# One VectorE instruction per modulation block, a later gate-bias scaling, and a fixed reuse order for two single buffers

## The chip, the cores and the metric

The kernel runs on one NeuronCore of a Trainium2 chip. The metric is the time of one execution in microseconds of device time. The median of three runs of the kernel before is 3478.86 us (3476.70 to 3480.21).

TensorE (PE in the profile) does matrix products and transposes, VectorE (DVE) and ScalarE (ACT) elementwise work, GpSimd (POOL) a little elementwise work, and SyncE (SP) issues nearly all transfers between HBM and the on-chip memory. Each engine runs its own instructions in the order in which they were written.

## The reference

Two networks follow each other on one sequence of 512 tokens with 1024 features. The first has two layers of: a hybrid mixer (branches A and B are attention, branch C is spatial gating), cross attention to a memory, and a convolutional feed-forward. The second has two layers with a mixer and an MLP each; both are wrapped in a modulation computed from a vector `c`. What the change touches:

```python
def window_attention(...):            # branch A; B is the dense form without the band
    p = jax.nn.softmax(jnp.concatenate([s, sink_l], axis=-1), axis=-1)[..., :-1]
    o = jnp.einsum('bnkgqs,bnskd->bnqkgd', p, vw)

def hybrid_mixer(...):
    gates = jax.nn.sigmoid(gate + b_gate)              # b_gate is the gate bias
    merged = (jnp.einsum('bsnc,ncd->bsnd', branches, w_branch) * gates).sum(axis=2)

def sandwich(x, c_act, sublayer, g_pre, g_post, w_mod, b_mod):
    shift, scale, gate = jnp.split(c_act @ w_mod + b_mod, 3, axis=-1)
    h = rms_norm_2(x, g_pre) * (1 + scale) + shift
    return x + gate * rms_norm_2(sublayer(h), g_post)
```

`c_act @ w_mod` is a row vector of 1024 numbers times a matrix of 1024 x 3072, four times (two layers, two sublayers each). `diff_attention`, in the first mixer of the second network, subtracts one softmax from another for each of eight heads.

## The kernel before

**Precision.** Almost every product is done in three passes: weights and activations are each split into a high part (`whi`, `fTh`, a reduced format) and the rest (`wlo`, `fTl`), and three matmuls of 128 x 512 add up hi x hi, hi x lo and lo x hi (`mm3`). A weight block of 128 x 1024 numbers arrives by DMA in `raw` (three buffers); ScalarE copies it to `whi`, VectorE subtracts to get `wlo` (`split_block`; six buffers of each).

**Order.** The kernel is traced through a recording layer (`Line`, L133 to L279) that keeps an estimate of when each engine is free and each tile ready. `defer` puts a piece of work on a heap with the estimated time at which its inputs are ready, and `poll`, called after every triple of matmuls, runs what is due. So the instruction order of every engine follows from the estimated costs in `cost` (L262): a VectorE `scalar_tensor_tensor` is booked at 0.13 us + n/960, a GpSimd elementwise operation at 0.07 us + n/460. `pump` splits weight blocks ahead of their use as long as VectorE is not booked too far ahead. All instructions pass through one helper line, so the profile puts them all on L186.

**The modulation** (`mod_load`, `mod_step`, `mod_go`, L1274 to L1330) is worked off inside the two feed-forwards (`conv_ffn`), 48 blocks in each: every up-projection of the feed-forward triggers one or two steps. A step takes one block of 128 x 1024 numbers of the matrix (`mraw`, three buffers, loaded two steps ahead). For the first of eight blocks ScalarE writes `macc = mraw * c`. For the other seven ScalarE scales `mraw` in place by a number per partition and GpSimd adds it to `macc`. After the eighth, `sums` has TensorE add up the 128 partitions with a matrix of ones (`macc,ones`), twelve times in all.

**The gate bias.** `hybrid` loads `bg` (128 x 24) and halves it on VectorE at once. Its first use is the `Tanh` in `branch`, after branch C and the projections of branch A.

**Attention of branches A and B, and the sliding window later** (`launch`, `probs_out`). Sixteen units run in pairs; each pair turns its probabilities (`sc`) by TensorE transposes into `pt0` and `pt1`, one buffer each, and then multiplies them by the values (`pv`). Nothing in the plan orders the turning of one pair after the `pv` of the pair before. In the same way `diff` has one buffer `qkl` for the low part of a head's keys, which the score products of the head read.

Of the kernel before, what the change touches and what calls it, by code (L numbers as in the profile page):

```python
# [14 lines left out]
AF = mybir.ActivationFunctionType  # L15
# [288 lines left out]
class KB:  # L304
# [460 lines left out]
    def probs_out(self, pool, u):  # L765


        nc, sh = self.nc, u.shared
        if not sh:
            sh["pt"] = [self.tile(pool, (P, u.wide // P, 2, P), f"pt{e}") for e in range(2)]  # L770
            sh["ev"] = Event(2, lambda: self.defer(0, pv, *sh["pt"]))
        for e in range(2):
            pp = self.ps((P, 4, P))
            self.transpose4(pp, [u.sc[e][:, b * P:b * P + P] for b in range(u.nkb)])
            pt = sh["pt"][e][:, :u.nkb, u.pr, :]
            if e == 0:
                nc.scalar.activation(pt, pp[:, :u.nkb, :], AF.Copy)
            else:
                nc.vector.tensor_copy(pt, pp[:, :u.nkb, :])
        u.read.set()  # L780

        def pv():
            po = self.ps((P, 2 * P))
            vc = slice(64 * u.kv, 64 * u.kv + 64)
            for b in range(u.nkb):
                for e in range(2):
                    nc.tensor.matmul(po[64 * e:64 * e + 64, :], lhsT=u.v[:, u.b0 + b, vc],
                                     rhs=sh["pt"][e][:, b, :, :].rearrange("p r q -> p (r q)"),
                                     start=b == 0, stop=b == u.nkb - 1)
            self.poll()  # L790
            sl, k = slice(u.i * P, u.i * P + P), 2 * u.kv
            self.split(u.br.h[:, k:k + 2, sl], u.br.l[:, k:k + 2, sl], po.rearrange("p (r q) -> p r q", r=2))

        sh["ev"].set()

# [55 lines left out]
    def launch(self, pool, unit, step, br, **kw):  # L851


        units, depth = [], kw["bufs"] // 2

        def start(n):
            if n >= depth and not units[n - depth].read.done:
                units[n - depth].read.after(lambda: self.defer(0, lambda: start(n)))
                return
            unit(pool, units[n])  # L860

        for n in range(16):
            kv, i, pr = n // 8, n // 2 % 4, n % 2
            u = Unit(kv=kv, i=i, pr=pr, shared={} if pr == 0 else units[-1].shared, br=br, read=Event(),
                     **{k: v for k, v in kw.items() if k != "band"})
            u.b0, u.nkb, u.add = kw["band"](i)
            units.append(u)
            self.defer(n * step, lambda n=n: start(n), kw["kh"], kw["kl"])


    def hybrid(self, l, xT):
        nc, A = self.nc, self.A
        with self.pool("hp") as hp:
            W = Weights(self, "w_in", l)
            WB = Weights(self, "w_branch", l)
            bg = self.load(hp, A["b_gate"][l], (P, 24), "bg")
            nc.vector.tensor_scalar_mul(bg, bg, 0.5)
            mg = self.tile(hp, (P, KD, S), "mg")

            def branch(n, br, first, done=None):  # L880
                wb = None
                for m in range(KD):
                    c = n * 8 + m
                    ps = self.dense(W.next(), 0, xT, KD)
                    gt = self.tile(hp, (P, S), "gt", 2)
                    nc.scalar.activation(gt, ps, AF.Tanh, bias=bg[:, c:c + 1], scale=0.5)
                    if m % 2 == 0:
                        wb = WB.next()
                    ps = self.dense(wb, (m % 2) * P, br, 4, keep=m % 2 == 0)
                    if first:  # L890
                        nc.vector.scalar_tensor_tensor(mg[:, m, :], gt, 1.0, ps, op0=ALU.add, op1=ALU.mult)
                    else:
                        nc.vector.scalar_tensor_tensor(gt, gt, 1.0, ps, op0=ALU.add, op1=ALU.mult)
                        nc.vector.tensor_tensor(mg[:, m, :], mg[:, m, :], gt, op=ALU.add)
                    if done:
                        done(m)

            def new_br():
                return FT(*self.pair(hp, (P, 4, S), "br", 2))

            brc = new_br()
            with self.pool("cp") as cp:
                self.branch_c(cp, l, xT, W, brc)
                self.flush()
            bra = new_br()
            with self.pool("ap") as ap, ExitStack() as es:
                self.branch_ab(es, ap, l, xT, W, bra, "a")
                branch(2, brc, True)
                self.flush()
            brb = new_br()  # L910
            with self.pool("ap") as ap, ExitStack() as es:
                self.branch_ab(es, ap, l, xT, W, brb, "b")
                branch(0, bra, False)
                self.flush()
            with self.pool("mt") as mt:
                hi, lo = self.pair(mt, (P, KD, S), "mT")
                mT = FT(hi, lo, (), [Event() for _ in range(KD)])

                def merged(m):
                    def go():  # L920
                        self.split(hi[:, m, :], lo[:, m, :], mg[:, m, :], scale=0.5)
                        mT.ev_k[m].set()
                    self.defer(0, go, mg[:, m, :])

                branch(1, brb, False, merged)
                self.flush_to_k(mT)
                self.open_boundary(self.open_right(), A["ln1_g"], A["ln1_b"], l)
                WM = Weights(self, "w_mix_out", l)
                fT, after = self.ln_start()
                self.tok(WM, mT, KD, 512, lambda t, ps: self.residual(t, 0, ps), by_k=True)  # L930
                self.tok(WM, mT, KD, 512, lambda t, ps: (self.residual(t, 1, ps), after(t)))
        return fT
# [356 lines left out]
    def mod_go(self):  # L1289
        nc, i = self.nc, self.mod_todo[0]  # L1290
        if not self.planning and nc.ready(self.mod_raw[i]) > self.now():
            self.defer(0, self.mod_go, self.mod_raw[i])
            return
        self.mod_todo.pop(0)
        s, kind, k = self.mod_steps[i]
        self.mod_load(i + 2)
        raw = self.mod_raw.pop(i)
        ck = self.cact[:, k:k + 1]
        if k == 0:
            self.mod_acc = self.tile(self.mod_pool, (P, D), "macc", 2)  # L1300
            nc.scalar.activation(self.mod_acc, raw, AF.Copy, scale=ck)
        else:
            nc.scalar.activation(raw, raw, AF.Copy, scale=ck)
            nc.gpsimd.tensor_tensor(self.mod_acc, self.mod_acc, raw, op=ALU.add)
        if k == KD - 1:
            acc, row = self.mod_acc, self.mod_sums[kind][s]

            def sums():
                ps = self.ps()
                for j in range(4):  # L1310
                    self.mm(ps[32 * j:32 * j + 32, 0:256], self.ones[:, 0:32], acc[:, 256 * j:256 * j + 256], 256)
                r = self.tile(self.mod_pool, (P, 256), "msum", 2)
                nc.scalar.activation(r, ps[:, 0:256], AF.Copy)
                nc.sync.dma_start(row.rearrange("(j c) -> j c", j=4), r[0:128:32, :])
                if c_last:
                    self.mod_finish(self.mod_pool)
                self.mod_left.set()

            c_last = i == len(self.mod_steps) - 1
            self.defer(0, sums, acc)  # L1320
# [415 lines left out]
    def diff(self, dp, hT, W, v, yT):  # L1736
        nc, A = self.nc, self.A
        sub = self.load(dp, A["e_diff_norm"], (P, 1), "sub")
        nc.vector.tensor_scalar_mul(sub, sub, 1.0 - LAM_INIT)

        def head(h):
            T = self.tile(dp, (P, 512), "T", 2)
            self.toeplitz(T, h, 0, 512)
            qk = []
            shared = {}

            def unit(i):
# [3 lines left out]
                for m in range(2):  # L1751
# [3 lines left out]
                    nc.vector.tensor_tensor_reduce(s, ps[:, :Wd], T[:, 384 - i * P:512], 1.0, NEG,  # L1755
                                                   ALU.add, ALU.max, mx[:, m:m + 1])
                    s2.append(s)
                nc.vector.tensor_scalar_mul(nm_, mx, -1.0)
                for m in range(2):
                    nc.scalar.activation(s2[m], s2[m], AF.Exp, bias=nm_[:, m:m + 1], accum_out=sums[:, m:m + 1])  # L1760
# [49 lines left out]
            def ev(i, ps):  # L1810
                t = self.tile(dp, (P, 2, S), f"qk{i}", 2, F32R)
                qk.append(t)
                if i == 0:
                    self.stack_q([t[:, e, :] for e in range(2)], ps, HD ** -0.5)
                else:
                    qk.append(self.tile(dp, (P, 2, S), "qkl", 1, F32R))
                    self.stack_k(t, qk[2], ps)
                    for n in range(NT):
                        self.defer(2.0 * n, lambda n=n: unit(n), *qk)
# [294 lines left out]
```

## Time and profile before

| quantity | before |
|---|---|
| median of three runs | 3478.86 us |
| the profiled execution, its own time | 3478.01 us |
| its span, first to last instruction | 3476.2 us |
| PE busy | 3366.9 us (97%) |
| DVE busy | 2078.5 us (60%) |
| ACT busy | 1433.7 us (41%) |
| POOL busy | 347.3 us (10%) |
| granted TensorE clock, mean | 0.987 of full |

The span is 1.8 us shorter than the execution's own time, and that execution lies within 0.03% of the median. "Busy" counts time in which at least one instruction of the engine is in flight. A row of the waits says which engine stood idle, for which tile it was released, and by whose work. "PEclk" is the share of TensorE's full clock that was granted in a stretch: 1.00 is 2.4 GHz, 0.50 is 1.2 GHz.

### The profile page before, as it was taken

To read this page: it belongs to the slowest core of one execution; us is meant where nothing else is said; L and a number is where in the kernel's file an instruction comes from. 1 tells how busy PE (TensorE), PEld (TensorE's weight loads), DVE (VectorE), ACT (ScalarE), POOL (GpSimd) and SP (SyncE) were. 2 spreads that over 40 slices of the span, in tenths; PEclk is the share of its full clock that TensorE was granted. 3 is DMA by queue.
4 is the path that set the end of the run, shared out by engine and by line. 5 is a ranking of instruction groups with operands and counts; after the bars stand their busy time and mean duration, and the time that the engine had idled before them with its cause. 6 is when DMAs were issued, how large, how long until landed. Compare 5 with 4: busy or idle time off the path is not lost. (4 is left out here: it accounts for less than half of the span.)

```text
span 3476.2 us, 42309 instructions
## 1 busy us (share of the span) xinstructions
PE 3366.9 (97%) x16500; PEld 2749.0 (79%) x16500; DVE 2078.5 (60%) x3370; ACT 1433.7 (41%) x2497; POOL 347.3 (10%) x250
## 2 busy tenths in 40 slices
PE   8999999999999999999999899999999999999999
PEld 6887887777778878887777678777888887888887
DVE  5767467665667674676656666487433466553334
ACT  3544334544335452444543343475332344433222
POOL 0010001432200100013322000001000010010000
PEclk9999999999999999999999999999999999999999
DMA  4221445644332224445443221313322331333222
GB/s 147 70 69 60 143 155 181 207 164 145 118 118 70 72 67 140 158 177 182 162 153 118 86 79 55 100 49 136 104 97 97 121 111 55 103 138 109 93 95 87
DMA packets 116760, 399.24 MB, mean 115 GB/s; under 512 B 14608, under 2 KB 18592, under 8 KB 116560
## 3 DMA queue, kind: packets, MB, share of 16 engines
q1 hardware_dynamic: 115984, 394.44, 33.4%
q8 instruction: 130, 2.13, 0.2%
q0 software_dynamic: 576, 2.10, 0.2%
q14 instruction: 70, 0.57, 0.1%
HBM read 375.39 MB, written 23.71 MB: 115 GB/s over the span
## 5 line engine op out<-in xcount | busy, mean ns | idle before, releaser
L186 DVE TENSOR_TENSOR wlo<-raw,whi 128x1024 fp32r<-128x1024 f32 x531 | 716.5, 1354 | 688.5 <-ACT whi L186 678.4
L186 PE MATMUL bank<-fTh,whi 128*128 128x512 f32 (+1 forms) x2320 | 886.8, 382 | 0.0
L186 PE MATMUL bank<-fTl,whi 128*128 128x512 f32 (+1 forms) x2320 | 872.4, 376 | 0.4
L186 PE MATMUL bank<-fTh,wlo 128*128 128x512 f32 (+1 forms) x2320 | 871.8, 376 | 0.1
L186 ACT ACTIVATE whi<-raw 128x1024 fp32r<-128x1024 f32 x531 | 553.6, 1047 | 379.2 <-PE bank L186 345.8
L186 PEld LDWEIGHTS bank<-fTh,whi 128*128 128x128 f32 x2320 | 441.4, 190 | 90.5 <-issue 10.5
L186 PEld LDWEIGHTS bank<-fTh,wlo 128*128 128x128 f32 x2320 | 441.0, 190 | 85.4 <-DVE wlo L186 0.5
L186 PEld LDWEIGHTS bank<-fTl,whi 128*128 128x128 f32 x2320 | 441.5, 190 | 79.8 <-DVE fTl L186 1.3
L186 PE MATMUL bank<-whi,gh 128*128 128x512 f32 x864 | 343.2, 397 | 0.0
L186 PE MATMUL bank<-whi,gl 128*128 128x512 f32 x864 | 342.5, 396 | 0.0
L186 PE MATMUL bank<-wlo,gh 128*128 128x512 f32 x864 | 342.4, 396 | 0.0
L186 POOL TENSOR_TENSOR macc<-macc,mraw 128x1024 f32<-128x1024 f32 x84 | 225.9, 2690 | 449.2 <-ACT mraw L186 448.0
L186 PE MATMUL bank<-whi,fTh 128*128 128x512 f32 (+2 forms) x608 | 231.5, 381 | 12.8 <-ACT whi L186 7.1
L186 PE MATMUL bank<-wlo,fTh 128*128 128x512 f32 (+2 forms) x608 | 224.1, 369 | 9.9 <-DVE wlo L186 9.9
L186 PE MATMUL bank<-whi,fTl 128*128 128x512 f32 (+2 forms) x608 | 223.7, 368 | 0.5 <-DVE fTl L186 0.5
L186 PEld LDWEIGHTS bank<-whi,gh 128*128 128x128 f32 x864 | 163.1, 189 | 40.1 <-issue 0.8
L186 PEld LDWEIGHTS bank<-wlo,gh 128*128 128x128 f32 x864 | 163.2, 189 | 39.4
L186 PEld LDWEIGHTS bank<-whi,gl 128*128 128x128 f32 x864 | 162.9, 188 | 39.5
L186 POOL TENSOR_TENSOR rstd<-rstdv,mhalf 128x1 f32<-128x1 f32 x68 | 56.5, 832 | 1053.1 <-DVE rstdv L186 1050.5
L186 DVE SCALAR_TENSOR_TENSOR y<-bank,cv,y 128x511 f32<-128x511 f32 x176 | 131.3, 747 | 37.2 <-ACT y L186 34.1
L186 PEld LDWEIGHTS bank<-whi,fTh 128*128 128x128 f32 x608 | 115.9, 191 | 33.7 <-ACT whi L186 8.8
L186 PEld LDWEIGHTS bank<-wlo,fTh 128*128 128x128 f32 x608 | 116.0, 191 | 29.7 <-DVE wlo L186 12.3
(322 smaller groups left out, 4649.4 us busy)
## 6 DMA issues: line engine op xcount, KB each, us to landing
raw<-in_mlp_w_dram SPq DMA_DIRECT2D x128, 512.0 KB, 3.3
mraw<-in_mod_w_dram SPq DMA_DIRECT2D x96, 512.0 KB, 4.7
raw<-in_w_in_dram SPq DMA_DIRECT2D x88, 512.0 KB, 3.3
raw<-in_f_w_up_dram SPq DMA_DIRECT2D x88, 512.0 KB, 4.2
raw<-in_e_w_in_dram SPq DMA_DIRECT2D x48, 512.0 KB, 4.1
raw<-in_f_w_down_dram SPq DMA_DIRECT2D x40, 512.0 KB, 3.5
raw<-in_o_w_in_dram SPq DMA_DIRECT2D x30, 512.0 KB, 4.3
raw<-in_w_branch_dram SPq DMA_DIRECT2D x24, 512.0 KB, 3.3
```

What stands on the lines that cost most here:

```text
L186: r = f(*a, **k)
```

## The change

Four edits. The seven steps per sum that were a ScalarE scaling and a GpSimd addition become one VectorE instruction, `macc = mraw * c + macc`. The halving of `bg` is issued after branch C. `probs_out` of a pair is held back until the `pv` of the pair before has been issued (events `before` and `over`). In `diff`, a head waits, before it takes the buffer `qkl`, for the score units of the head before to be issued.

```diff
@@ probs_out
+        if not u.before.done:
+            u.before.after(lambda: self.defer(0, lambda: self.probs_out(pool, u)))
+            return
...
             self.split(u.br.h[:, k:k + 2, sl], u.br.l[:, k:k + 2, sl], po.rearrange("p (r q) -> p r q", r=2))
+            u.over.set()
@@ launch
+            u.before, u.over = (units[-1].before, units[-1].over) if pr else (units[-1].over if units else Event(0), Event())
@@ hybrid
             bg = self.load(hp, A["b_gate"][l], (P, 24), "bg")
-            nc.vector.tensor_scalar_mul(bg, bg, 0.5)
...
                 self.branch_c(cp, l, xT, W, brc)
+                nc.vector.tensor_scalar_mul(bg, bg, 0.5)
                 self.flush()
@@ mod_go
         else:
-            nc.scalar.activation(raw, raw, AF.Copy, scale=ck)
-            nc.gpsimd.tensor_tensor(self.mod_acc, self.mod_acc, raw, op=ALU.add)
+            nc.vector.scalar_tensor_tensor(self.mod_acc, raw, ck, self.mod_acc, op0=ALU.mult, op1=ALU.add)
@@ diff
+        scored = [Event(0)]
...
+            before, now = scored[-1], Event(NT)
+            scored.append(now)
...
+                now.set()
...
+                    self.wait(before)
                     qk.append(self.tile(dp, (P, 2, S), "qkl", 1, F32R))
```

The order on VectorE at the program's start, before: `bg` is the gate bias, `raw` a weight block, `fTl` and `wlo` the low parts of the turned input and of the weights.

```order
L186 TENSOR_SCALAR bg_114<-bg_114 128x24
L186 TENSOR_TENSOR fTl_93<-bank_25_133,fTh_92 128x4x128
L186 TENSOR_TENSOR fTl_93<-bank_26_140,fTh_92 128x4x128
L186 TENSOR_TENSOR wlo_148<-raw_99,whi_147 128x1024
L186 TENSOR_TENSOR fTl_93<-bank_30_156,fTh_92 128x4x128
L186 TENSOR_TENSOR fTl_93<-bank_31_163,fTh_92 128x4x128
```

The order on VectorE at the same place now:

```order
L186 TENSOR_TENSOR fTl_93<-bank_25_132,fTh_92 128x4x128
L186 TENSOR_TENSOR fTl_93<-bank_26_139,fTh_92 128x4x128
L186 TENSOR_TENSOR wlo_147<-raw_99,whi_146 128x1024
L186 TENSOR_TENSOR fTl_93<-bank_30_155,fTh_92 128x4x128
L186 TENSOR_TENSOR fTl_93<-bank_31_162,fTh_92 128x4x128
L186 TENSOR_TENSOR wlo_170<-raw_103,whi_169 128x1024
```

The `bg` instruction is gone from the head of the queue; it now stands some fifty rows later, behind the third gated group of branch C. The split of the second weight block has moved up, ahead of the other input tiles.

The order on VectorE in the first feed-forward's up-projection, before (`y` is a convolved projection, `gl` the low part of the gated product):

```order
L186 SCALAR_TENSOR_TENSOR y_1117_5657<-bank_1109_5613,cv_5078,y_1117_5657 128x511 x2
L186 TENSOR_TENSOR wlo_5682<-raw_5552,whi_5681 128x1024
L186 TENSOR_TENSOR y_1117_5657<-y_1108_5608,y_1117_5657 128x512
L186 TENSOR_TENSOR gl_5696<-y_1117_5657,gh_5695 128x512
L186 SCALAR_TENSOR_TENSOR y_1126_5705<-bank_1118_5661,cv_5078,y_1126_5705 128x511 x2
L186 TENSOR_TENSOR wlo_5724<-raw_5588,whi_5723 128x1024
```

The order on VectorE at the same place now:

```order
L186 SCALAR_TENSOR_TENSOR y_1121_5684<-bank_1113_5640,cv_5078,y_1121_5684 128x511 x2
L186 SCALAR_TENSOR_TENSOR macc_5616<-mraw_5605,cact,macc_5616 128x1024
L186 SCALAR_TENSOR_TENSOR macc_5616<-mraw_5614,cact,macc_5616 128x1024
L186 TENSOR_TENSOR wlo_5722<-raw_5595,whi_5721 128x1024
L186 SCALAR_TENSOR_TENSOR y_1128_5727<-bank_1122_5689,cv_5078,y_1128_5727 128x511 x2
L186 TENSOR_TENSOR wlo_5745<-raw_5638,whi_5744 128x1024
L186 SCALAR_TENSOR_TENSOR macc_5616<-mraw_5699,cact,macc_5616 128x1024
L186 TENSOR_TENSOR y_1128_5727<-y_1121_5684,y_1128_5727 128x512
L186 TENSOR_TENSOR gl_5758<-y_1128_5727,gh_5757 128x512
```

The modulation's instructions now stand between the weight splits and the convolution, one or two at a time.

The order on TensorE at the first of the twelve sums, before:

```order
L186 MATMUL bank_1109_5613<-fTl_4855,whi_5493 128x512
L186 MATMUL bank_1109_5613<-fTh_4854,wlo_5494 128x512
L186 MATMUL bank_1115_5646<-macc_5269,ones 32x256 x4
L186 MATMUL bank_1109_5613<-fTh_4854,whi_5493 128x512
L186 MATMUL bank_1109_5613<-fTl_4855,whi_5493 128x512
```

The order on TensorE at the same sum now:

```order
L186 MATMUL bank_1113_5640<-fTl_4855,whi_5591 128x512
L186 MATMUL bank_1113_5640<-fTh_4854,wlo_5592 128x512
L186 MATMUL bank_1114_5650<-macc_5269,ones 32x256 x4
L186 MATMUL bank_1113_5640<-fTh_4854,whi_5591 128x512
L186 MATMUL bank_1113_5640<-fTl_4855,whi_5591 128x512
```

The sum still stands in the middle of an up-projection, twelve rows later in TensorE's list.

## Rows read from the trace of the kernel before

**Rows 1.** The page, part 1: busy time, share, instructions of each engine.
```profile
PE 3366.9 (97%) x16500; PEld 2749.0 (79%) x16500; DVE 2078.5 (60%) x3370; ACT 1433.7 (41%) x2497; POOL 347.3 (10%) x250
```

**Rows 2.** Waits of PE: waiter, what for, total us, times, longest.
```profile
PE bank L186 <- POOL macc L186: 36.5, 12, 5.1
...
PE bank L186 <- DVE wlo L186: 9.9, 5, 6.1
```

**Rows 3.** Windows by stage: length, busy per engine, PEclk, DMA share, GB/s.
```profile
24.30:560.00 535.70, 533.52 (x2821) 437.15 (x2822) 349.16 (x694) 225.81 (x447) 25.50 (x29) 1.00 0.30 102
560.00:900.00 340.00, 323.36 (x1486) 260.95 (x1484) 218.92 (x204) 160.05 (x193) 112.16 (x42) 0.97 0.53 183
...
1510.00:1850.00 340.00, 321.51 (x1467) 259.61 (x1465) 215.33 (x202) 161.95 (x195) 112.85 (x43) 0.97 0.50 175
```

**Rows 4.** Timeline of PE around the first sum: start, length, instruction, [idle before].
```profile
623.57 0.64 PE L186 MATMUL bank<-macc,ones 128*32 128x256 f32 x8 [3.22 <-POOL macc L186]
...
625.16 0.63 PE L186 MATMUL bank<-fTh,wlo 128*128 128x512 f32 x1
625.59 0.63 PE L186 MATMUL bank<-fTh,whi 128*128 128x512 f32 x1
...
627.65 0.39 PE L186 MATMUL bank<-fTh,wlo 128*128 128x512 f32 x1
627.88 0.39 PE L186 MATMUL bank<-fTh,whi 128*128 128x512 f32 x1
```

**Rows 5.** Windows of the eight half-clock stretches behind sums: first, and all together.
```profile
624.15:627.56 3.41, 3.41 (x12) 2.76 (x9) 1.54 (x2) 3.41 (x5) 0.00 (x0) 0.50 0.50 154
...
sum 40.96, PE 34.16 PEld 24.67 DVE 26.86 ACT 21.79 POOL 8.81; mean PE 4.27 PEld 3.08 DVE 3.36 ACT 2.72 POOL 1.10
```

**Rows 6.** Groups of POOL by shape, whole trace: count, busy, mean ns, idle before.
```profile
L186 POOL TENSOR_TENSOR macc<-macc,mraw 128x1024 f32<-128x1024 f32 x84 | 225.9, 2690 | 449.2 <-ACT mraw L186 448.0
```

**Rows 7.** Groups of ACT by shape, from 560 to 1860 us.
```profile
L186 ACT ACTIVATE mraw<-mraw,cact 128x1024 f32<-128x1024 f32 x84 | 94.9, 1138 | 0.0
```

**Rows 8.** Groups of DVE by shape, whole trace.
```profile
L186 DVE SCALAR_TENSOR_TENSOR y<-y,mv,gb 128x1024 f32<-128x1024 f32 x24 | 30.6, 1274 | 0.0
...
L186 DVE COPY pt<-bank 128x512 f32<-128x512 f32 x32 | 21.9, 685 | 6.0 <-PE bank L186 6.0
```

**Rows 9.** Groups of DVE by shape in the first feed-forward, 582 to 903 us.
```profile
L186 DVE TENSOR_TENSOR wlo<-raw,whi 128x1024 fp32r<-128x1024 f32 x53 | 101.9, 1925 | 68.3 <-ACT whi L186 65.1 <-DMA mraw<-in_mod_w_dram 3.0
L186 DVE SCALAR_TENSOR_TENSOR y<-bank,cv,y 128x511 f32<-128x511 f32 x76 | 56.7, 747 | 9.5 <-ACT y L186 8.1
L186 DVE TENSOR_TENSOR y<-y,y 128x512 f32<-128x512 f32 x19 | 24.0, 1263 | 0.0
```

**Rows 10.** The same in the second feed-forward, 1530 to 1851 us.
```profile
L186 DVE TENSOR_TENSOR wlo<-raw,whi 128x1024 fp32r<-128x1024 f32 x53 | 100.5, 1900 | 70.0 <-ACT whi L186 69.7
```

**Rows 11.** The same after 2440 us, without modulation work.
```profile
L186 DVE TENSOR_TENSOR wlo<-raw,whi 128x1024 fp32r<-128x1024 f32 x167 | 204.3, 1224 | 315.7 <-ACT whi L186 314.4
L186 DVE TENSOR_TENSOR gl<-r,gh 128x512 fp32r<-128x512 f32 x64 | 44.3, 692 | 44.7 <-ACT gh L186 44.7
L186 DVE TENSOR_TENSOR r<-r 128x512 f32<-128x512 f32 x64 | 43.8, 684 | 0.0
```

**Rows 12.** Timeline of the start, 13 to 16.5 us: VectorE and SyncE's issue.
```profile
13.44 0.18 DVE L186 TENSOR_SCALAR bg<-bg 128x24 f32<-128x24 f32 x1 [10.32 <-DMA bg<-in_b_gate_dram]
...
14.73 1.21 DVE L186 TENSOR_TENSOR wlo<-raw,whi 128x1024 fp32r<-128x1024 f32 x1
15.97 0.33 SPq L186 DMA_DIRECT2D raw<-in_w_in_dram  x1
```

**Rows 13.** Timeline of ACT at the start.
```profile
8.02 1.05 ACT L186 ACTIVATE whi<-raw 128x1024 fp32r<-128x1024 f32 x1
```

**Rows 14.** Windows of the start; columns as in Rows 3.
```profile
15.00:16.00 1.00, 0.00 (x1) 0.00 (x1) 0.94 (x1) 0.00 (x0) 0.00 (x0) 1.00 0.17 64
...
17.00:19.20 2.20, 2.20 (x12) 2.18 (x11) 0.46 (x1) 0.83 (x2) 0.00 (x0) 1.00 0.67 229
```

## The prediction, made before the changed kernel ran

> **What bounds the kernel now.** I read the page's busy times first: TensorE is busy 97% of the span, VectorE 60% [rows 1]. So only two things can change the time by much: the moments in which TensorE stands idle, and the rate at which it works. The table of TensorE's waits comes next [rows 2]. One line dominates it: twelve waits for `macc`, 36.5 us together, each released by GpSimd. There are twelve sums of the modulation, so every sum makes TensorE wait, 3.0 us on average. The second view is the table by stage [rows 3]: TensorE idles 2.2 us in the 536 us before the first feed-forward, but 16.6 and 18.5 us in the two feed-forward stretches, and there alone of these rows the granted clock is below 1.00 (0.97). The third view is TensorE's timeline around a sum [rows 4]. After 3.22 us of idling, the full-width matmuls start 0.43 us apart (625.16 to 625.59) where they start 0.23 us apart a little later (627.65 to 627.88). The clock rows agree [rows 5]: after eight of the twelve stalls there is a stretch at 0.50, which is 1.2 GHz, 40.96 us in all, in which TensorE was busy 34.16 us. A stall therefore costs twice: its own length, and the slow work after it.
>
> Why the waits are there can be read from the durations. The order was planned with a GpSimd addition at 0.07 + 1024/460 = 2.30 us; the trace shows 2.69 us [rows 6]. Seven additions follow each other in a sum, so the last is about 7 x 0.39 = 2.7 us later than the plan thinks, near the measured 3.0.
>
> **The modulation step.** Removed: 84 scalings on ScalarE of 1.138 us [rows 7], which leave an engine that does not bound, so I count nothing; and 84 additions on GpSimd. Added: 84 instructions of 128 x 1024 on VectorE with two inputs in on-chip memory and one number per partition. The trace has the same operation on the same shape at 1.274 us [rows 8]; I take 1.28, so 84 x 1.28 = 107.5 us more. VectorE also gets time back. While GpSimd adds, VectorE's two-input operations are slow: the weight split takes 1.925 and 1.900 us in the two feed-forwards [rows 9, 10] against 1.224 later [rows 11]; the product `y,y` takes 1.263 us [rows 9] against 0.684 for a product of that size [rows 11]. With GpSimd silent that returns 53 x 0.70 + 53 x 0.68 = 73 us on the splits and, taking the second feed-forward like the first, 38 x 0.58 = 22 us on the products. Net, VectorE carries about 12 us more in 680 us. Four gains and costs follow.
>
> First, the waits for `macc`. The new instruction is booked at 0.13 + 1024/960 = 1.20 us against my 1.28, so a sum is planned almost when it is ready. I leave 0.25 us per sum, 3 us; the bounds are 0 and one whole instruction per sum, 12 x 1.28 = 15 us. Gain 36.5 - 3 = 33.5 us.
>
> Second, the clock. At a spacing of 0.43 instead of 0.23 us, 34.16 us of busy time would have been 34.16 x 0.23/0.43 = 18.3 us; the gain is 15.8 us if all eight stretches go. Upper bound: half of 34.16, 17 us. Lower: 12 us, if two of the eight stay.
>
> The Trainium skill, "TensorE: Matmul & The Clock Gate", section "HAM oscillation — how this bites in real kernels", counts the penalty as throttled time x (1 - 1.2/2.4). By that the eight stretches would cost 20.5 us, 4.7 more than I take. The rows say less, because in 6.8 us of the 40.96 TensorE was still standing in the stall, which the first gain has already counted [rows 5].
>
> Third, new waits. The new instruction stands in VectorE's queue, in order, ahead of weight splits; behind a split waits TensorE, and behind a freed `raw` buffer SyncE's next load. The step also waits for its own load; today ScalarE, which reads that tile, never idles ahead of it (0.0 in its row [rows 7]), and the buffer is now released by one engine instead of two, so I expect none there. For the load on VectorE I count a round of four up-projections: four splits, eight convolution steps of 0.747, two products, two low parts of 0.692, and five modulation steps: 4.9 + 6.0 + 1.4 + 1.4 + 6.4 = 20.1 us [rows 9, 11], while TensorE needs 96 x 0.23 = 22.1 us. That fits, with 2 us to spare, so short waits where two steps come together are likely. Before, in the same place, VectorE was kept as busy by GpSimd, and TensorE did not wait for splits: 9.9 us in the whole trace [rows 2]. Bounds: 0, and the whole net load of 12 us. I take 5 us. A gain here is excluded, as there is next to nothing to win.
>
> **The gate bias.** At the start VectorE stands 10.32 us in front of `bg`, whose load is queued behind the input and three weight blocks, and everything else of VectorE is behind it [rows 12]. Without it the first weight block's low part, for which ScalarE's copy ends at 9.07 [rows 13], is done at 9.07 + 1.21 = 10.3 instead of 15.94 us: 5.7 us earlier. It also frees the buffer for the fourth block, whose load is issued at 15.97 now. The first burst of transfers ends soon after 15 us and that load then runs in 17 to 19.2 us [rows 14]; issued at 10.3 it queues behind the burst, so it gains at least 2.5 us. Bounds: 2.5 us and the whole wait, 10.3. I take 5.7. The moved instruction stands where the load landed long ago, so it costs its 0.18 us on an engine with room. If that cover were missing, the price would be a wait of the same kind, and only the gate's ScalarE work behind it would be late.
>
> **The two reuse orders.** In `diff` TensorE's order is unchanged for all eight heads, so I count nothing. In the attention of the hybrid stages the turning of a pair's probabilities now comes after the values product of the pair before. What hides this is the dense stream between: TensorE idles only 2.2 us there [rows 3], so no more than that can be won per layer. If the stream did not cover it, each of at most 35 such orders (five launches, seven each) would cost one copy of 0.685 us [rows 8], 24 us. I take 0, the nearer row being the 2.2 us of idling.
>
> **The sum.** 33.5 + 15.8 - 5 + 5.7 = 50.0 us. The profiled execution took 3478.0 us, 0.9 below the median of the runs: 3478.0 - 50.0 = 3428 us, 1.5% faster.
>
> **Rivals.**
> *VectorE becomes late.* The sums and the splits wait for VectorE, since five extra instructions per round leave 2 us of slack. For: the slack is thin, and instructions come in twos. Against: the splits lose 0.7 us each, and VectorE's net load hardly rises. Price, with every bound at its bad end: 15 us of sum waits stay, 12 us of clock return, 12 us of split waits are new, and 2.5 us at the start are won: 36.5 - 15 + 12 - 12 + 2.5 = 24 us, so 3454 us.
>
> *VectorE bounds the up-projections: slower than before.* This is decided by the length of the new instruction. There are 96/5 = 19 rounds. To lose the other gains (33.5 + 15.8 + 5.7 = 55 us), a round must exceed TensorE's 22.1 us by 2.9 us, so the instruction must take (22.1 + 2.9 - 13.7)/5 = 2.3 us. At GpSimd's 2.69 us for the same shape a round would be 27.2 us: 19 x 5.1 = 97 us lost, 3478 - 55 + 97 = 3520 us. For: no row shows this instruction itself. Against: the same operation on this shape takes 1.274 us wherever GpSimd is quiet [rows 8]. The Trainium skill, "Perfetto Trace Analysis", section "Optimizing Scalar/DVE Operations", speaks on this side: work of a saturated VectorE is better moved to ScalarE or GpSimd, and this change does the reverse. The same passage warns that these two share a read port, so that moving work between them might not help; the slow splits next to GpSimd's additions [rows 9, 11] agree with the warning.
>
> *The wait was for something else.* The releaser is inferred. If the sums wait for another thing that ends at the same time, the 36.5 us stay and only the start moves: 3478 - 5.7 = 3472 us. Against it: the plan's error of 2.7 us fits the waits.
>
> **How the numbers follow.** The forecast has a chance of 0.78, its own range is 3415 (all gains at their upper ends, no new wait: 36.5 + 17 + 10.3 = 64) to 3440 us. VectorE late: 0.13. The wait was for something else: 0.05. VectorE bounds: 0.04. The range for 8 in 10 is 3414 to 3445 us, which takes in the better half of the second case. About 0.2% (7 us) is what a measurement of this kernel can tell from no change. Faster by more: the first two cases, 0.91. The third case, at 0.18%, is within: 0.05. Slower: 0.04.
>
> **What would show it.** Right: GpSimd's busy time falls to about 121 us and ScalarE's to about 1338; the wait for `macc` falls below 5 us with VectorE as releaser; the granted clock in both feed-forward stretches is 1.00 or nearly; the weight split there takes 1.22 us; the new instruction takes 1.28 us; the dense stream of the start is under way some 5 us earlier. Wrong: waits of TensorE for `wlo` in the feed-forwards over 12 us, a new instruction above 1.5 us, stretches at half clock that stay behind the sums, or new idle time in the hybrid stages.

## The result and the profile after

The changed kernel takes 3426.05 us (median of four runs, 3418.82 to 3426.46) against 3477.78 us for the kernel before (median of four, one run more than ahead of the prediction): a ratio of 0.9846, with a 95% interval of 0.9829 to 0.9863. The forecast was 3428 us, in a range of 3414 to 3445.

The profiled execution is the fastest of the four, 3418.82 us with a span of 3417.1 us. Its busy times (page, part 1; before in [rows 1]):

```profile
PE 3347.9 (98%) x16500; PEld 2731.1 (80%) x16500; DVE 2080.5 (61%) x3454; ACT 1349.2 (39%) x2411; POOL 121.1 (4%) x166
```

TensorE's idle time is span less busy: 3476.2 - 3366.9 = 109.3 us before, 3417.1 - 3347.9 = 69.2 us after, 40.1 less. Its busy time fell by 19.0 us for the same 16500 matmuls, so it worked at a higher rate. VectorE got 84 instructions more and is busy just 2 us longer.

The waits of TensorE (answering [rows 2]; waiter, what for, total us, times, longest): no line with `macc` is left.

```profile
PE bank L186 <- DVE ss L186: 14.2, 3, 4.9
PE bank L186 <- ACT whi L186: 8.0, 4, 3.6
PE bank L186 <- DVE y L186: 7.3, 9, 1.7
PE bank L186 <- DVE wlo L186: 5.4, 9, 1.0
```

The windows by stage (answering [rows 3]; moved to where the stages now lie; length, busy of PE, PEld, DVE, ACT, POOL, PEclk, DMA share, GB/s). The two feed-forward stretches, where TensorE stood 16.6 and 18.5 us, now have under 2 us of idling each, and the granted clock is 1.00.

```profile
24.00:556.00 532.00, 529.19 (x2803) 432.34 (x2802) 345.95 (x692) 221.34 (x443) 25.47 (x29) 1.00 0.30 100
556.00:890.00 334.00, 332.27 (x1555) 268.73 (x1554) 231.74 (x260) 127.68 (x162) 1.41 (x1) 1.00 0.56 191
...
1478.00:1810.00 332.00, 330.04 (x1544) 267.38 (x1543) 227.93 (x257) 124.51 (x158) 1.42 (x1) 1.00 0.52 180
```

Both gains can be read over the same matmuls of the two feed-forwards (575.02 to 915.36 and 1525.01 to 1860.31 us before, 571.14 to 885.96 and 1494.67 to 1804.00 us after). The sums of the two windows are 675.64 us before (first line) and 624.15 us after (second line). TensorE stood for 0.25 us of it instead of 36.52, and was busy for 623.90 us instead of 639.12.

```profile
sum 675.64, PE 639.12 PEld 510.53 DVE 424.78 ACT 322.15 POOL 225.93; mean PE 319.56 PEld 255.26 DVE 212.39 ACT 161.07 POOL 112.97
...
sum 624.15, PE 623.90 PEld 500.05 DVE 425.02 ACT 238.46 POOL 0.00; mean PE 311.95 PEld 250.03 DVE 212.51 ACT 119.23 POOL 0.00
```

TensorE's timeline around the first sum (answering [rows 4]): the sum starts in the running stream, no idle time stands behind it in brackets, and the matmuls after it are 0.23 us apart at once (620.22, 620.45, 620.68), where before they were 0.43 us apart.

```profile
618.99 0.40 PE L186 MATMUL bank<-fTh,wlo 128*128 128x512 f32 x1
619.31 0.64 PE L186 MATMUL bank<-macc,ones 128*32 128x256 f32 x8
619.88 0.50 PE L186 MATMUL bank<-fTh,whi 128*128 128x512 f32 x1
620.22 0.39 PE L186 MATMUL bank<-fTl,whi 128*128 128x512 f32 x1
620.45 0.39 PE L186 MATMUL bank<-fTh,wlo 128*128 128x512 f32 x1
620.68 0.39 PE L186 MATMUL bank<-fTh,whi 128*128 128x512 f32 x1
```

VectorE's groups in the first feed-forward (answering [rows 9]; count, busy us, mean ns, idle before): the weight split is back from 1.925 to 1.224 us, the product `y,y` from 1.263 to 0.685 us, and the new instruction takes 1.278 us.

```profile
L186 DVE TENSOR_TENSOR wlo<-raw,whi 128x1024 fp32r<-128x1024 f32 x57 | 69.6, 1224 | 44.4 <-ACT whi L186 43.1 <-DMA ms<-msum 1.3
...
L186 DVE SCALAR_TENSOR_TENSOR macc<-mraw,cact,macc 128x1024 f32<-128x1024 f32 x42 | 53.7, 1278 | 1.5 <-DMA mraw<-in_mod_w_dram 1.4
L186 DVE TENSOR_TENSOR y<-y,y 128x512 f32<-128x512 f32 x22 | 15.1, 685 | 0.0
```

The start (answering [rows 12]): the first block's low part is computed at 8.54 us instead of 14.73, and the fourth block's load is issued at 10.91 us instead of 15.97.

```profile
8.54 1.23 DVE L186 TENSOR_TENSOR wlo<-raw,whi 128x1024 fp32r<-128x1024 f32 x1 [0.25 <-ACT whi L186]
...
10.91 0.33 SPq L186 DMA_DIRECT2D raw<-in_w_in_dram  x1
```

### The profile page after: what moved, and what is told of

The parts are those of the page before. It is cut to its first block, busy times and chain, and to the rows that moved or that the text cites. A ratio compares the mean times of both kernels' runs of the same rounds, so it can differ in the third digit from the quotient of the medians.

```text
span 3417.1 us, 42048 instructions
## 1 busy us (share of the span) xinstructions
PE 3347.9 (98%) x16500; PEld 2731.1 (80%) x16500; DVE 2080.5 (61%) x3454; ACT 1349.2 (39%) x2411; POOL 121.1 (4%) x166
## 5 line engine op out<-in xcount | busy, mean ns | idle before, releaser
L186 DVE TENSOR_TENSOR wlo<-raw,whi 128x1024 fp32r<-128x1024 f32 x531 | 642.4, 1214 | 632.0 <-ACT whi L186 622.9
L186 PEld LDWEIGHTS bank<-whi,fTh 128*128 128x128 f32 x608 | 116.0, 191 | 33.8 <-ACT whi L186 10.4
L186 PEld LDWEIGHTS bank<-whi,fTl 128*128 128x128 f32 x608 | 115.7, 190 | 20.9 <-DVE fTl L186 1.2
L186 DVE TENSOR_TENSOR y<-y,bank 128x512 f32<-128x512 f32 x96 | 64.9, 684 | 110.7 <-PE bank L186 110.5
```

Of the source, the lines that this page charges most:

```text
L186: r = f(*a, **k)
```

## The experiments

The theory: TensorE pays for sums that the plan puts too early, twice, by standing and by working at half clock afterwards; the new instruction ends that because its booked cost is nearly right. (Why the plan put the sums too early turned out otherwise; see the end of the second experiment.) The main rivals: VectorE's freedom from GpSimd is what counts, or another part of the change is.

### The parts alone: modulation, gate bias, reuse orders

The edits are the parts of the change's diff: the first kernel has the one line of `mod_go`, the second the moved line of `hybrid`, the third the events in `probs_out`, `launch` and `diff`; the rest is as before.

> The kernel before with the modulation step on VectorE alone. My theory (TensorE no longer waits for the twelve sums, and its clock no longer falls behind them): it gives nearly the whole gain of the change less the start, 36.5 us of waits and 16 us of clock less about 5 us of new waits, so 3426 to 3434 us. Rival (the new order of the attention pairs carries a good part): 3440 us or more.

> The kernel before with the gate bias halved later, alone. My theory: the start gains 5.6 us (the idle time of TensorE in the first 25 us falls from 15.0 to 9.4) and nothing gives it back: 3472 us, ratio 0.9984. Rival (a stage later waits for a transfer that comes no earlier, and the gain is gone by then): 3478 us.

> The kernel before with the two reuse orders alone. My theory: no change, 3478 us within 3 us, TensorE's idle time in the hybrid stages as before (about 2 us each). Rival (holding a pair back leaves TensorE without work): 3483 us or more; other rival (the copies no longer hold up ScalarE): 3473 us.

| kernel | median us | ratio to before | 95% interval |
|---|---|---|---|
| modulation alone | 3424.97 | 0.9846 | 0.9833 to 0.9860 |
| gate bias alone | 3471.61 | 0.9980 | 0.9971 to 0.9989 |
| reuse orders alone | 3479.39 | 1.0002 | 0.9993 to 1.0011 |

The modulation alone gives as much as the whole change, the bias alone gives its 7 us, and the reuse orders give nothing. The modulation alone came out 1 us below the range of its first theory; the other two fit theirs, and the rival that the attention order carries the gain falls. With the reuse orders alone TensorE idles 3.1 and 2.7 us in the two hybrid windows against 2.2 and 2.2 before, so a cost of about 1 us cannot be excluded. The bias's 7 us are not all won at the start: in the first 25 us TensorE is busy 15.00 us instead of 9.95, 5 us more, and in the same profile the sums' waits are 33.8 us instead of 36.5, which the modulation on VectorE removes anyway. Even so, 54 and 5 us are more than the whole change gained (below).

### Is it the engine or the place of the sums?

Here ScalarE and GpSimd keep the modulation, and only the twelve sums are planned later:

```diff
-            self.defer(0, sums, acc)
+            self.defer(0, lambda: self.defer(4.5, sums), acc)
```

> The kernel before, with ScalarE and GpSimd still doing the modulation, but each of the twelve sums planned 4.5 us later (it then stands 21 rows later on TensorE, about 4.8 us, against stalls of at most 5.1 us). My theory (what costs is only that the sums stand too early): nearly the whole gain comes without touching the engine, 3478 - 36 - 16 = 3426 us, splits on VectorE still slow at 1.9 us. Rival (it is VectorE's freedom from GpSimd that counts): 3470 us or more.

Measured: 3437.78 us, ratio 0.9884 (0.9870 to 0.9897). It is nearer to the theory, but 12 us off. The wait for `macc` (same view and columns as above) has not gone to zero:

```profile
PE bank L186 <- POOL macc L186: 9.4, 4, 4.8
```

The longest, 4.78 us at 661 us, is the second sum. TensorE, not held up at the first sum any more, reaches the second one earlier by what it saved, and GpSimd is no faster. A smaller delay, 2.5 us in the same line, was meant to separate the price of standing from that of the clock:

> The kernel before with each sum planned 2.5 us later (12 rows, about 2.8 us). The stalls were 0.7 to 5.1 us long; about 11 us of the 36.5 should stay, none over 2.4 us. My theory (a stall has two prices, and the clock's is paid only behind the longer ones): the waits give 25 us and the half-clock stretches behind the sums vanish almost all, 16 us more: 3437 us. Rival (only the waits count): 3453 us. Rival (the clock is lost in proportion to the waits): 25 + 11 us, 3442 us.

Measured: 3455.16 us, ratio 0.9930 (0.9917 to 0.9942). The number lies next to a rival, "only the waits count", but the trace does not bear that rival out. The waits fell by much less than planned, for the same reason as above:

```profile
PE bank L186 <- POOL macc L186: 22.8, 8, 6.2
```

So the dose was not the one intended. What the run can still tell is the sum of both prices. Its page has a span of 3453.4 us with TensorE busy for 3356.6 us, against 3476.2 and 3366.9 before: 12.5 us less idle time and 10.3 us less busy time for the same 16500 matmuls, 22.8 us together. The clock's records agree: 24.2 us less at half clock (65.1 against 89.3), where TensorE loses 1 - 0.23/0.43 = 0.46 of the stretch, make 11.1 us. The waits alone would be little more than half.

The clean test came with 10 us:

> The kernel before, ScalarE and GpSimd still doing the modulation, each sum planned 10 us later instead of 4.5. The 4.5 us left five stalls (9.4 us) because TensorE, no longer held up at one sum, reaches the next one earlier. My theory (only the place of the sums costs): no wait for macc is left, the splits on VectorE stay slow (1.9 us), and the time is that of the modulation on VectorE alone, 3425 us within 4. Rival (GpSimd's hold on VectorE costs the other 13 us by itself): 3435 us or more.

Measured: 3425.83 us, ratio 0.9856 (0.9841 to 0.9870); the kernel with the modulation on VectorE alone, run beside it, took 3425.43 us. No `macc` line is left among TensorE's waits. The groups of VectorE in the first feed-forward show its splits as slow as ever, and the window (columns as in [rows 3]) shows GpSimd as busy as before and TensorE idle for 1.7 us:

```profile
L186 DVE TENSOR_TENSOR wlo<-raw,whi 128x1024 fp32r<-128x1024 f32 x55 | 103.8, 1889 | 61.9 <-ACT whi L186 61.6
```
```profile
560.00:900.00 340.00, 338.28 (x1581) 273.46 (x1580) 231.94 (x221) 168.61 (x205) 114.33 (x43) 1.00 0.55 189
```

One constant in the plan gives the same time as moving the work to another engine. This settles it: the place of the sums cost the 50 us, and neither GpSimd's length nor VectorE's slow splits by themselves.

It does not tell why the plan had put the sums too early, as a delay cures any lateness. The prediction read it from seven additions in a row that each take 0.39 us longer than booked. The trace of the kernel before shows another chain. In eight of the twelve sums GpSimd stands idle for 3.5 to 6.5 us ahead of the last addition, until ScalarE has scaled the block, so that no lateness of the additions before it is left; that last addition takes 2.34 to 2.41 us where 2.30 are booked. (In the other four, two additions follow each other.) The scaling stands in ScalarE's queue behind `gh` or `y`, which wait for VectorE. For the first sum, rows of VectorE, ScalarE and GpSimd:

```profile
612.68 2.69 DVE L186 TENSOR_TENSOR wlo<-raw,whi 128x1024 fp32r<-128x1024 f32 x1 [1.97 <-ACT whi L186]
...
616.73 2.00 DVE L186 TENSOR_TENSOR wlo<-raw,whi 128x1024 fp32r<-128x1024 f32 x1
618.65 0.68 DVE L186 TENSOR_TENSOR y<-y,y 128x512 f32<-128x512 f32 x1
...
619.36 0.63 ACT L186 ACTIVATE gh<-y 128x512 fp32r<-128x512 f32 x1 [4.06 <-DVE y L186]
619.90 1.13 ACT L186 ACTIVATE mraw<-mraw,cact 128x1024 f32<-128x1024 f32 x1
...
621.18 2.34 POOL L186 TENSOR_TENSOR macc<-macc,mraw 128x1024 f32<-128x1024 f32 x1 [3.54 <-ACT mraw L186]
```

The two splits take 2.69 and 2.00 us beside GpSimd's additions, where `cost` books 0.07 + 1024/960 = 1.14 us each: 2.4 us late, against a stall of 3.2. By this estimate most of the stall goes back to VectorE's slow splits, by way of the place of the sum. It is read from the trace; no run here gives the plan the slow splits' true cost.

### How much more VectorE can bear

Two kernels add one instruction each to every step of the changed kernel's modulation: the first a second VectorE instruction, the second a GpSimd addition. Both write into the block that has just been used and that nothing reads again, so what is computed stays the same. The fence shows the two edits one below the other; the comments name the runs.

```diff
             nc.vector.scalar_tensor_tensor(self.mod_acc, raw, ck, self.mod_acc, op0=ALU.mult, op1=ALU.add)
+            nc.vector.scalar_tensor_tensor(raw, raw, ck, raw, op0=ALU.mult, op1=ALU.add)   # twice on VectorE
...
+            nc.gpsimd.tensor_tensor(raw, raw, raw, op=ALU.add)                              # GpSimd beside
```

> The changed kernel with a second instruction of the same form and shape behind each modulation step; its result is not used. This doubles what VectorE got. My count: a round of four up-projections needs 20.1 + 6.4 = 26.5 us of VectorE against 22.1 of TensorE, 19 rounds x 4.4 = 84 us, so 3510 us, with TensorE waiting for weight splits. Rival (the splits run so far ahead that a round may be longer, the down-projections make it up): below 3445 us.

> The changed kernel with a GpSimd addition of 128x1024 behind each modulation step; nothing uses its result. TensorE waits for nothing of GpSimd. My theory: VectorE's two-input operations are slow again (splits 1.9 us, the modulation instruction about 2 us), a round needs about 20.1 + 5 x 1.1 = 25.7 us of VectorE, and TensorE waits for splits: 19 x 3.6 = 68 us, 3494 us. Rival (GpSimd gives way, or the splits run far enough ahead): 3426 to 3435 us.

Twice on VectorE: 3483.37 us, ratio 1.0011 (1.0001 to 1.0020). The change's whole gain is gone, but the loss is 57 us where I counted 84. TensorE's waits show it where it was expected, behind the splits, and on ScalarE. Its copies (`whi`) are late because they stand in its queue behind `y` and `gh`, for which ScalarE itself waits for VectorE: in the feed-forwards all the waits for `whi` over 1 us have this chain. The two totals, and one such copy:

```profile
PE bank L186 <- ACT whi L186: 32.7, 18, 3.2
PE bank L186 <- DVE wlo L186: 24.6, 30, 2.9
```
```profile
650.72 0.63 ACT L186 ACTIVATE y<-y 128x512 f32<-128x512 f32 x1 [1.66 <-DVE y L186]
651.26 1.04 ACT L186 ACTIVATE whi<-raw 128x1024 fp32r<-128x1024 f32 x1
...
652.35 0.50 PE L186 MATMUL bank<-fTh,whi 128*128 128x512 f32 x1 [1.82 <-ACT whi L186]
```

GpSimd beside: 3461.32 us, ratio 0.9948 (0.9933 to 0.9963): 35 us above the change, where I counted 68. The rival, that GpSimd would give way or the splits run far enough ahead, is refuted. The groups of VectorE in the first feed-forward show which operations pay:

```profile
L186 DVE TENSOR_TENSOR wlo<-raw,whi 128x1024 fp32r<-128x1024 f32 x54 | 86.8, 1611 | 31.0 <-ACT whi L186 30.8
L186 DVE SCALAR_TENSOR_TENSOR y<-bank,cv,y 128x511 f32<-128x511 f32 x80 | 59.6, 745 | 10.3 <-ACT y L186 8.9
L186 DVE SCALAR_TENSOR_TENSOR macc<-mraw,cact,macc 128x1024 f32<-128x1024 f32 x42 | 56.8, 1353 | 0.1
L186 DVE TENSOR_TENSOR gl<-y,gh 128x512 fp32r<-128x512 f32 x20 | 27.5, 1375 | 14.0 <-ACT gh L186 14.0
```

The low part `gl` doubles (0.693 to 1.375 us), the split takes 1.611 us, the new instruction, behind which GpSimd starts, hardly changes, and the convolution step, with one input in PSUM (the memory that takes TensorE's results), not at all (0.749 to 0.745 us). The splits were expected at 1.9 us and the modulation instruction at 2 us, so the slowing was smaller than forecast. TensorE does not pay at the splits alone. The largest line of its waits that is new against the changed kernel is that for the sums, although GpSimd no longer works on them:

```profile
PE bank L186 <- DVE macc L186: 12.7, 6, 3.6
```

Here too the plan knows nothing of VectorE's slow operations and puts the sums too early, which agrees with the chain read above. So VectorE keeps up with the plan only because GpSimd fell silent: the two halves of that edit belong together. How much of the 35 us a later place of the sums would give back was not tested. Over the feed-forwards' matmuls (624.15 us in the changed kernel) the two runs took 686.19 and 665.29 us; TensorE stood for 41 and 30 us of it and was busy for 21 and 12 us longer, which the counts of 84 and 68 us, made of standing alone, leave out. Why it stands so much less than counted was not tested; the count leaves out that splits can run ahead of a round.

### Where the gate bias's gain goes

> The changed kernel without its two reuse orders (modulation on VectorE and the gate bias later). My theory (the parts add: 54 us of the modulation, 6 to 7 of the start, reuse orders 0): 3418 us, and the changed kernel in the same job the same within 3 us. Rival (the reuse orders cost something once the rest is faster): the changed kernel is slower than this by 5 us or more.

> The changed kernel once more, beside its parts on the same chip. If the parts add: 3418 to 3420 us, 5 to 7 us below the modulation alone. Rival (what the start gains is given back once the modulation is on VectorE): 3425 us, as the modulation alone.

> The kernel before with the modulation on VectorE alone, once more, beside the whole change on the same chip: 3425 us. Both theories say this; it is the yardstick for the two runs before it.

| kernel, run side by side, four runs each | median us | lowest to highest |
|---|---|---|
| modulation and bias, no reuse orders | 3422.13 | 3419.53 to 3423.64 |
| the whole change | 3424.24 | 3423.34 to 3426.08 |
| modulation alone | 3425.43 | 3423.12 to 3429.01 |

The first kernel was expected at 3418 us and missed that by 4; the whole change missed its 3418 to 3420 us by 4 as well. The ranges of the last two overlap, so the rival, that the start's gain is given back, is the nearer: of the 7 us hardly anything can be seen in the whole change. The windows of the first 25 us (same columns) show that the gain at the start itself is there in the whole change (first fence), against the modulation alone (second fence): TensorE is busy 14.91 us instead of 10.42.

```profile
1870.40:1885.40 15.00, 10.03 (x40) 8.11 (x40) 12.78 (x14) 7.07 (x11) 2.65 (x2) 0.77 0.40 136
1968.50:1983.50 15.00, 11.74 (x54) 9.42 (x54) 8.77 (x13) 6.38 (x13) 0.00 (x0) 0.77 0.42 137
2125.00:2140.00 15.00, 12.98 (x62) 10.84 (x62) 9.91 (x13) 7.79 (x12) 0.00 (x0) 0.89 0.41 135
0.00:25.00 25.00, 14.91 (x60) 10.80 (x61) 11.86 (x18) 11.82 (x17) 0.69 (x6) 1.00 0.75 265
```
```profile
1873.50:1888.50 15.00, 10.11 (x44) 8.06 (x44) 13.02 (x15) 7.08 (x11) 2.64 (x2) 0.89 0.41 140
1970.50:1985.50 15.00, 11.45 (x58) 9.38 (x58) 8.80 (x14) 7.21 (x16) 0.00 (x0) 0.89 0.42 138
2126.10:2141.10 15.00, 12.98 (x68) 10.66 (x68) 9.72 (x13) 7.57 (x12) 0.00 (x0) 1.00 0.48 164
0.00:25.00 25.00, 10.42 (x47) 8.14 (x48) 9.80 (x17) 10.86 (x15) 0.69 (x6) 1.00 0.60 218
```

The other three rows of each fence lie behind the same three stalls in the first mixer of the second network, ahead of its `diff`, where nothing in the change touches the order. After stalls of similar length (4.01 and 3.68 us, 2.46 and 2.45, 2.02 and 2.02) the whole change gets a lower clock (0.77, 0.77, 0.89) than the modulation alone (0.89, 0.89, 1.00). In the page's busy times the whole change has 74.5 - 70.3 = 4.2 us less idle time (spans of 3422.9 and 3423.0 less busy times of 3348.4 and 3352.7) and is busy 4.3 us longer. In these two profiles the start's gain is given back as slower work at places without a connection to it. The kernel without the reuse orders has the same in its profile (68.6 us idle, 3353.3 us busy), so they are not the cause. The first profile of the whole change had the shorter stretches there and a span of 3417.1 us. So the gain at the start is shown, and that it is lost again in the clock of those two profiles too; that the runs without a profile lose it in the same way was not seen, and why a stall of one length is followed by more or less slow work stays open. Nor can four runs each say whether the reuse orders cost 2 us: alone no cost can be seen.

## Why the prediction was right, step by step

- *The waits for `macc`* were forecast to shrink from 36.5 to 3 us; none is left. That the place of the sums is what costs is borne out by the run with sums 10 us later, which corrects the place alone and gets the same time. The reason given for the place is not: seven additions of 0.39 us extra each made 2.7 us, near the measured 3.0, but this agreement is chance. The additions do not follow each other, and at the first sum, whose rows are shown, most of the delay comes from VectorE's slow splits. The term came out because the change ends that too: with GpSimd silent the splits take 1.224 us, near the 1.14 booked.
- *The clock* was put at 15.8 us. Over the feed-forwards' own matmuls TensorE's busy time fell by 15.2 us (639.12 to 623.90), and the second profile of the changed kernel gives the same 15.2 (623.89). In the whole program it fell by 19.0 us in the first profile and by 14.2 in the second (3352.7); that difference is the scatter of the stretches behind other stalls.
- *The other count of the clock.* The Trainium skill, "TensorE: Matmul & The Clock Gate", section "HAM oscillation — how this bites in real kernels", counts half of the throttled time, 20.5 us of the 40.96 here. The measured 15.2 us bear out the smaller count by spacing and busy time.
- *New waits for splits* were put at 5 us. This is the term that was mis-sized: between 24 us and 1850 us TensorE waits 1.2 us in all for `wlo`, in three waits, where it waited 2.4 us before.

```profile
PE bank L186 <- DVE wlo L186: 1.2, 3, 0.4
```

- *The round's count* (20.1 of 22.1 us) was right about there being room: the new instruction takes 1.278 us where 1.28 was taken. VectorE's busy time rose by 2 us where 12 were counted. About 5 us of the difference are other low parts that GpSimd had slowed as well (`gl` from 0.791 to 0.693 us, and the half-width splits); the rest is that neighbouring instructions overlap, which busy time counts once.
- *The gate bias* was put at 5.7 us. Alone it gives 7 us, of which 5 are won at the start. In the whole change TensorE gains 4.5 us in the first 25 us, which the clock gives back in the profile compared above.
- *The reuse orders* at 0: 1.0002, as forecast.
- *The signs.* GpSimd is busy for 121.1 us, as forecast; ScalarE for 1349.2 us where 1338 were forecast, without a cost, as it does not bound. None of the signs of being wrong is there.
- *The rivals.* That the wait was for something else falls with the waits themselves, and VectorE did not become late. VectorE as the bound needs an instruction of 2.3 us by the forecast's count. The run with two instructions of 1.28 us per step, 2.56 us together, is the test: it took 3483 us, as long as the kernel before or just longer (ratio 1.0001 to 1.0020), so the rival's mechanism is real, though it costs less than counted.
- *The advice on moving work.* The Trainium skill, "Perfetto Trace Analysis", section "Optimizing Scalar/DVE Operations", says that it may make sense to offload work from a saturated VectorE to ScalarE or GpSimd. At 60% busy VectorE was not saturated, and the run with the sums 10 us later, which leaves the work with ScalarE and GpSimd, takes the same time: here neither engine was the better place. The warning in the same passage, that VectorE and GpSimd share a read port, agrees with the slow splits beside GpSimd (1.925 us against 1.224) and with the 35 us that GpSimd's additions cost the changed kernel.

The median fell by 51.7 us against 50.0 forecast. That it is so near is in part luck: the feed-forwards alone gave 51.5 us (36.3 of standing, 15.2 of clock) where 33.5 + 15.8 - 5 = 44.3 were forecast, and most of the 5.7 us of the start was given back elsewhere.

## What to carry to other kernels

Where an order is planned from booked costs, look at the engine that bounds for a wait at every instruction of one kind: here twelve of 0.7 to 5.1 us, one at each sum, were an error in the plan, and planning that instruction later removed them without moving any work. Follow the chain behind such a wait back to the first instruction that ran longer than booked; it can be on another engine than the one that released the wait. Price a stall on TensorE twice, by its length and by the rows of the granted clock behind it. When one of two such waits is removed, expect the next one to grow, as the engine arrives there earlier.

## What had not been expected of the hardware

- The same program on the same inputs had spans of 3417.1 and 3423.0 us in two profiles, with nearly the same idle time of TensorE (69.2 and 70.3 us) but busy times of 3347.9 and 3352.7 us: the clock behind unchanged stalls differed.
- A GpSimd addition of 128x1024 that starts behind a VectorE instruction slows the two-input instructions that follow it, and hardly the one before: `gl` from 0.693 to 1.375 us, the split from 1.224 to 1.611 us, the modulation instruction from 1.278 to 1.353 us.
- At the first sum of the kernel before, that slowing reached TensorE by way of three engines: VectorE's splits of 2.69 and 2.00 us kept ScalarE waiting, ScalarE's scaling kept GpSimd waiting, and GpSimd's addition, itself only 0.04 us over its booked 2.30, released the sum 3.2 us late.
